# Down projection of a gated MLP: eight block products replaced by seven, with other loads and queues

## Chip, core and metric

One NeuronCore of a Trainium2 chip runs the whole program; the seven others do not take part. The metric is the device time of one execution in microseconds (us). Engines are named as in the profile: PE is TensorE (matmul), PEld its weight loads, DVE is VectorE, ACT is ScalarE, POOL is GpSimd, SP is SyncE, which here only issues DMAs.

## What is computed

One layer of a hybrid diffusion backbone for 2048 latent tokens and 128 context tokens with D_MODEL 1024 and D_FF 2816. A mixing sub-layer comes first, then a gated MLP. The change touches only the last two lines of the MLP:

```python
h = rmsnorm(x, g_pre_ffn) * (1.0 + scale_f) + shift_f
gt, up = jnp.split(h @ w_up, 2, axis=-1)
gt = (dwconv2d_grid(gt, conv_ffn) if grid else dwconv1d(gt, conv_ffn[1])) + b_conv_ffn
y = (jax.nn.silu(gt) * up) @ w_down          # (2176 x 2816) @ (2816 x 1024)
x = x + gate_f * rmsnorm(y, g_post_ffn)
```

All data is float32.

## The kernel before

The program is one `hybrid_step_kernel` that goes through five stages. Stages 1 to 3 (input projection, DeltaNet, output projection) end with `d_x2`, the residual stream, in DRAM. Stage 4 computes the up projection in two passes `p` over the two halves of the latent tokens, 22 column groups `j` in each. A `unit(p, j)` is seven products of 12 matmuls (a seven-product block scheme for `w_up`); `gate(p, j)` is the 3x3 depthwise convolution on DVE, SiLU on ACT and the product with the up branch, and it writes `d_y` (17 tiles of 128 tokens x 22 groups of 128 features) to DRAM. The operands of the unit lie in tiles T0 to T6 of 16 KB a partition, made in the order 0, 5, 4, 6, 1, 2, 3, which is also the order in which the last unit uses them for the last time.

Every float32 operand of a matmul is split into a high part (a copy rounded to float32r, by ACT) and a low part (a subtraction, by DVE or POOL), and one block product is three matmuls: high x high, high x low, low x high. One matmul has a 128x128 stationary piece of the activations and a 128x512 moving piece of the weights.

Stage 5 (lines 1463 to 1543) is the down projection and the end of the layer. `load_wd` (1469) makes the split weights of one k (128 rows of `w_down`, 512 columns) in 22 tiles `wd0` to `wd21`. `down_mm` (1475) takes a tile `c` of 128 tokens: for each half `q` of the 22 groups it loads 704 KB of `d_y` into `yt` (1478, SP's queue), splits it into `yr` (ACT 1480, DVE 1481), and issues 33 matmuls (1484 to 1486). The outer loop runs over the two column halves `hf`. For `hf` 0 the squares are summed (ACT 1524) and the result is copied to `half` (DVE 1526). For `hf` 1 all 22 weight tiles are made anew (loads 1512), and behind each token tile stand the root (1529), the reciprocal (1530), two scalings (DVE 1535, 1537), the addition of `d_x2` (loaded at 1533, added at 1539) and the store (1543, for the context tile 1541). All stage-5 DMAs are issued by SP. The first two token tiles use PSUM banks of stage 4, since the last `gate(1, 21)` is issued only after the split of tile 1 (`issue_after(last_v)`, 1497).

Tiles come from pools with a fixed number of buffers; a new use of a buffer waits for the last use of the old one. The framework writes the semaphores and puts the instructions of each engine in an order that it plans ahead, by program order and by the times that it expects; on the chip each engine and each queue then runs in that order.

## Time and profile before

| | us |
|---|---|
| median of three runs | 2793.51 (2789.07 to 2797.16) |
| the profiled execution | 2791.89 |
| its span (first to last instruction) | 2790.1 |
| stage 5: first to last matmul start | 2268.96 to 2781.93 |

| engine | busy us | share of the span | instructions |
|---|---|---|---|
| PE | 2654.8 | 95% | 15309 |
| DVE | 1907.2 | 68% | 2840 |
| ACT | 1153.1 | 41% | 2421 |
| POOL | 789.9 | 28% | 851 |

Matmuls are pipelined, so the duration of one in the records (391 ns) is longer than the distance from one to the next; where a rate is wanted, the starts are to be compared. A row of the timeline has the start, the duration, engine, line, operation, output <- inputs, and in brackets how long the engine had been idle and what ended that. PEclk is the granted clock of TensorE as a share of 2.4 GHz.

### The profile page before, as it was taken

The numbers are of one execution on the slowest core, as the hardware profiler recorded it, in microseconds if no ns is written. First come the engines' busy times: TensorE is split into PE (matmuls) and PEld (weight loads), VectorE is DVE, ScalarE is ACT, GpSimd is POOL, SyncE is SP. The second block draws the span as 40 slices with busy tenths as digits, with TensorE's granted clock in tenths as the row PEclk, the third lists the DMA queues.
The fourth block names the chain that finished last, engine by engine and source line by source line (L and its number), as shares of the span: only waits on it lengthen the run. The fifth ranks groups of instructions, "written<-read, shape, count | busy, mean of one in ns | idle before, by whom it ended". The sixth has DMA issues, their size and how long they took to land.

```text
span 2790.1 us, 41624 instructions
## 1 busy us (share of the span) xinstructions
PE 2654.8 (95%) x15309; PEld 2237.8 (80%) x15309; DVE 1907.2 (68%) x2840; ACT 1153.1 (41%) x2421; POOL 789.9 (28%) x851
## 2 busy tenths in 40 slices
PE   7999999979888998999899999999999999999998
PEld 4888888767778887888788888888888878888887
DVE  3898999885657785444687777887888873225343
ACT  5423132355656666666544444432222232224221
POOL 2211011166335683222666666500000000000000
PEclk9999999989969999999999999999999999999999
DMA  7024531576597565665777777888777754236453
GB/s 275 20 72 119 151 109 43 104 190 134 154 279 195 141 227 207 219 231 184 256 278 266 265 271 262 279 263 255 235 232 222 230 184 134 94 104 211 165 173 119
DMA packets 426712, 526.79 MB, mean 189 GB/s; under 512 B 144790, under 2 KB 301964, under 8 KB 426252
## 3 DMA queue, kind: packets, MB, share of 16 engines
q1 hardware_dynamic: 406380, 506.30, 57.5%
q10 hardware_dynamic: 20128, 17.83, 1.9%
q8 instruction: 121, 1.98, 0.3%
q14 instruction: 83, 0.68, 0.1%
HBM read 342.13 MB, written 181.90 MB: 188 GB/s over the span
## 4 chain that ended last, share of the span: by engine, by line
PE 61%; DMA 5%; DVE 4%; ACT 3%; SPq 3%; POOL 2%; issue 2%; ACTq 0%; DVEq 0%; POOLq 0%
PE ps L1318 10%; PE ps L1320 10%; PE ps L1319 10%; PE ps L1147 7%; PE ps L1486 6%; PE ps L1484 6%; PE ps L1485 6%; PE psc L1232 2%; SPq L166 1%; DVE dm L819 1%; PE p L938 1%; PE p L945 1%; DMA dm<-d_g 1%; DMA d_mix<-bigB 1%; PE p L957 1%
## 5 line engine op out<-in xcount | busy, mean ns | idle before, releaser
L1377 DVE SCALAR_TENSOR_TENSOR pa<-gb,pvf,pa 128x512 f32<-128x512 f32 (+1 forms) x704 | 491.0, 733 | 65.3 <-ACT pa L1375 62.5
L1318 PE MATMUL ps<-T,wr 128*128 128x512 f32 x1232 | 480.5, 391 | 0.1
L1319 PE MATMUL ps<-T,wr 128*128 128x512 f32 x1232 | 479.9, 389 | 0.0
L1320 PE MATMUL ps<-T,wr 128*128 128x512 f32 x1232 | 479.0, 390 | 0.6 <-POOL wr L1246 0.6
L361 PE MATMUL ps<-hH,wr 128*128 128x512 f32 (+1 forms) x960 | 349.7, 369 | 6.6 <-ACT bigA L412 3.8
L362 PE MATMUL ps<-hL,wr 128*128 128x512 f32 (+1 forms) x960 | 352.4, 367 | 0.0
L363 PE MATMUL ps<-hH,wr 128*128 128x512 f32 (+1 forms) x960 | 350.6, 366 | 0.0
L1484 PE MATMUL ps<-wd,yr 128*128 128x512 f32 x748 | 292.5, 391 | 6.1 <-ACT yr L1480 5.5
L1486 PE MATMUL ps<-wd,yr 128*128 128x512 f32 x748 | 292.1, 391 | 0.4 <-DVE yr L1481 0.4
L1485 PE MATMUL ps<-wd,yr 128*128 128x512 f32 x748 | 292.1, 391 | 0.0
L1318 PEld LDWEIGHTS ps<-T,wr 128*128 128x128 f32 x1232 | 231.4, 188 | 49.2 <-issue 0.8
L1320 PEld LDWEIGHTS ps<-T,wr 128*128 128x128 f32 x1232 | 231.4, 188 | 49.1 <-POOL wr L1246 1.1
L1319 PEld LDWEIGHTS ps<-T,wr 128*128 128x128 f32 x1232 | 231.4, 188 | 47.4
L375 DVE SCALAR_TENSOR_TENSOR acc<-bigA,pvt,acc 128x1024 f32<-128x1024 f32 (+2 forms) x168 | 252.3, 1502 | 13.2 <-ACT acc L372 9.2
L361 PEld LDWEIGHTS ps<-hH,wr 128*128 128x128 f32 x960 | 184.0, 193 | 33.5 <-ACT bigA L412 4.2
L1481 DVE TENSOR_TENSOR yr<-yt,yr 128x1408 fp32r<-128x1408 f32 x68 | 110.5, 1625 | 143.4 <-ACT yr L1480 143.3
L363 PEld LDWEIGHTS ps<-hH,wr 128*128 128x128 f32 x960 | 185.4, 193 | 25.4 <-issue 3.0
L362 PEld LDWEIGHTS ps<-hL,wr 128*128 128x128 f32 x960 | 185.3, 193 | 24.0 <-issue 1.6
L1351 POOL TENSOR_TENSOR up<-up,x 128x512 f32<-128x512 f32 x44 | 57.3, 1302 | 413.2 <-ACT pa L1383 217.9
L375 DVE SCALAR_TENSOR_TENSOR acc<-bigC,pvt,acc 128x1024 f32<-128x1024 f32 (+2 forms) x108 | 156.6, 1461 | 24.9 <-DMA bigB<-d_uc 15.5
L1484 PEld LDWEIGHTS ps<-wd,yr 128*128 128x128 f32 x748 | 141.0, 188 | 36.6 <-ACT yr L1480 6.5
L1486 PEld LDWEIGHTS ps<-wd,yr 128*128 128x128 f32 x748 | 141.0, 188 | 30.7 <-DVE yr L1481 1.4
(360 smaller groups left out, 4571.2 us busy)
## 6 DMA issues: line engine op xcount, KB each, us to landing
d_w<-wr SPq DMA_DIRECT2D x154, 512.0 KB
wr<-d_w SPq DMA_DIRECT2D x154, 512.0 KB
yt<-d_y SPq DMA_DIRECT2D x68, 704.0 KB
raw<-in_wup_dram SPq DMA_DIRECT2D x60, 512.0 KB
xt<-in_x_dram SPq DMA_DIRECT2D x34, 512.0 KB
wmt<-in_wmod_dram SPq DMA_DIRECT2D x24, 512.0 KB
wt<-in_win_dram SPq DMA_DIRECT2D x24, 512.0 KB
wmt<-in_wmod_dram SPq DMA_DIRECT2D x48, 256.0 KB
```

The source lines that it names most:

```text
L361: nc.tensor.matmul(ps[:, 0:n], wr[:, 0, k], hH[bi][:, k], start=(k == 0), stop=False)
L362: nc.tensor.matmul(ps[:, 0:n], wr[:, 0, k], hL[bi][:, k], start=False, stop=False)
L363: nc.tensor.matmul(ps[:, 0:n], wr[:, 1, k], hH[bi][:, k], start=False, stop=(k == KD - 1))
L375: nc.vector.scalar_tensor_tensor(dst, src[:, o + t:o + t + n], w[:, t:t + 1], dst, ALU.mult, ALU.add)
L1147: nc.tensor.matmul(pss[hf][:], a[:, k], w[k][:, 512 * hf:512 * hf + 512], start=(w is woH and a is mH and k == KD - 1), stop=(w is woL and ...
L1318: nc.tensor.matmul(ps[:], h, T[i][:, 0, k], start=(first and k == 0), stop=False, skip_group_check=True)
L1319: nc.tensor.matmul(ps[:], h, T[i][:, 1, k], start=False, stop=False, skip_group_check=True)
L1320: nc.tensor.matmul(ps[:], l, T[i][:, 0, k], start=False, stop=(k == HK - 1), skip_group_check=True)
L1377: nc.vector.scalar_tensor_tensor(rows(a), src, w[:, t:t + 1], rows(a), ALU.mult, ALU.add)
L1484: nc.tensor.matmul(ps[:], yr[:, 0, i], wd[:, 0], start=(q == 0 and i == 0), stop=False)
L1485: nc.tensor.matmul(ps[:], yr[:, 0, i], wd[:, 1], start=False, stop=False)
L1486: nc.tensor.matmul(ps[:], yr[:, 1, i], wd[:, 0], start=False, stop=(q == 1 and i == HN - 1))
```

## The change

The product Y W is cut into 2x2 blocks: Y by token half (tiles 0 to 7 and 8 to 15) and by half of the 22 groups, W by the same half of its rows and by column half. Seven products of sums and differences of blocks take the place of eight. The context tile belongs to the first token half and has no partner, so it takes part in products 1, 3, 5 and 7 only. The products run in the order 3, 1, 5, 6, 2, 4, 7; a unit `(i, c)` is one product for one token tile, 33 matmuls.

- `y_load` loads one or two blocks of `d_y` for a unit, each in two parts of 6 and 5 groups, two units ahead, on SP's queue into 8 buffers. `y_prep` adds or subtracts the two blocks (DVE) and splits (ACT, DVE), one unit ahead.
- `w_load` loads one or two 256 KB blocks of `w_down` per k, `w_make` adds or subtracts them (DVE) and splits (ACT; DVE or POOL). There are 15 weight buffers: 11 for the product that runs, 4 for the next. The other 7 are made as the last unit of a product frees them. From product 1 on, `w_load` is issued on POOL's queue into 3 buffers.
- `evict` copies (ACT) or adds or subtracts (DVE) the result of a unit into one or two of the accumulators `C1`, `C2` in SBUF.
- `final` has the work of the old lines 1524 to 1543, now from the accumulators, after each unit of product 4 (tiles 8 to 15) and of product 7 (tiles 0 to 7 and the context tile). The additions of `d_x2` go to POOL, but for tile 7 and the context tile, and the stores to POOL's queue.
- The pool `sp4` of stage 4 is closed after the first pass.

```diff
+        yq = s5.enter_context(tc.tile_pool(name="yq", bufs=8, reuse_waits="tile"))
+        yp = s5.enter_context(tc.tile_pool(name="yp", bufs=4, reuse_waits="tile"))
+        wpa = s5.enter_context(tc.tile_pool(name="wp5a", bufs=15, reuse_waits="tile"))
...
+        YS = {1: ((0, 0), (1, 1), ADD), 2: ((1, 0), (1, 1), ADD), 3: ((0, 0),), 4: ((1, 1),),
+              5: ((0, 0), (0, 1), ADD), 6: ((1, 0), (0, 0), SUB), 7: ((0, 1), (1, 1), SUB)}
+        WS = {1: ((0, 0), (1, 1), ADD), 2: ((0, 0),), 3: ((0, 1), (1, 1), SUB), 4: ((1, 0), (0, 0), SUB),
+              5: ((1, 1),), 6: ((0, 0), (0, 1), ADD), 7: ((1, 0), (1, 1), ADD)}
+        CS = {3: ((0, 1, None), (1, 1, None)), 1: ((0, 0, None), (1, 1, ADD)), 5: ((0, 0, SUB), (0, 1, ADD)),
+              6: ((1, 1, ADD),), 2: ((1, 0, None), (1, 1, SUB)), 4: ((0, 0, ADD), (1, 0, ADD)), 7: ((0, 0, ADD),)}
+        ORDER = (3, 1, 5, 6, 2, 4, 7)
+        units = [(i, c) for i in ORDER for c in list(range(8)) + ([CTX] if i in (1, 3, 5, 7) else [])]
+        KA = 6
+        PARTS = ((0, KA), (KA, HN - KA))
...
+        def y_prep(u):
+            yrs[u] = []
+            for (k0, kn), ts in zip(PARTS, yts.pop(u)):
+                if len(ts) == 2:
+                    nc.vector.tensor_tensor(ts[0], ts[0], ts[1], YS[u[0]][2])
+                yr = yp.tile([P, 2, KA, P], F32R, name="yr", tag="yr")
+                nc.scalar.copy(yr[:, 0, 0:kn], ts[0])
+                v = nc.vector.tensor_tensor(yr[:, 1, 0:kn], ts[0], yr[:, 0, 0:kn].bitcast(F32), SUB).ins
...
+        def w_load(i, k):
+            ws = wsp[0].tile([P, KD, P], F32, name="raw", tag="raw")[:].rearrange("p (a b) c -> p a (b c)", a=2)
+            t = [x for x in WS[i] if type(x) is tuple]
+            if len(t) == 2 and t[0][0] == t[1][0]:
+                wq[0].dma_start(ws, wdown[t[0][0] * HN + k].rearrange("p (a c) -> p a c", a=2))
+            else:
+                for n, (kh, h) in enumerate(t):
+                    wq[0].dma_start(ws[:, n], wdown[kh * HN + k, :, 512 * h:512 * h + 512])
...
+        def w_make(i, k, eng):
+            ws = wss.pop((i, k))
+            if len(WS[i]) == 3:
+                nc.vector.tensor_tensor(ws[:, 0], ws[:, 0], ws[:, 1], WS[i][2])
+            wd = wpa.tile([P, 2, 512], F32R, name="wd", tag="wd")
+            nc.scalar.copy(wd[:, 0], ws[:, 0])
+            eng.tensor_tensor(wd[:, 1], ws[:, 0], wd[:, 0].bitcast(F32), SUB)
...
+        y_load(units[0])
+        y_load(units[1])
+        y_prep(units[0])
+        AH = 3
+        for k in range(AH):
+            w_load(3, k)
+        for k in range(HN):
+            if k + AH < HN:
+                w_load(3, k + AH)
+            w_make(3, k, nc.vector if k % 2 == 0 else nc.gpsimd)
...
+        def final(t):
+            square(t, 0)
+            nc.vector.tensor_tensor(ss[:, t, 2:3], ss[:, t, 0:1], ss[:, t, 1:2], ADD)
+            nc.scalar.activation(ss[:, t, 3:4], ss[:, t, 2:3], AF.Sqrt, scale=1.0 / D, bias=epsb[:])
+            nc.vector.reciprocal(ss[:, t, 3:4], ss[:, t, 3:4])
+            xt = xts.pop(t)
+            G = Gs
+            if t == CTX:
+                G = fo.tile([P, D], F32, name="xt5", tag="xt5")
+                nc.sync.dma_start(G[:], d_gm[1][:, D:2 * D].to_broadcast([P, D]))
+            for h in range(2):
+                sl = slice(512 * h, 512 * h + 512)
+                nc.vector.scalar_tensor_tensor(C[h][:, t], C[h][:, t], ss[:, t, 3:4], G[:, sl],
+                                               ALU.mult, ALU.mult)
+                (nc.vector if t in (7, CTX) else nc.gpsimd).tensor_tensor(xt[:, sl], xt[:, sl], C[h][:, t], ADD)
+            nc.gpsimd.dma_start(y_prompt[0] if t == CTX else y_sample[0, t * P:(t + 1) * P, :], xt[:])
...
+        FREE = 15 - HN
+        wq[0] = nc.gpsimd
...
+        for n in range(3, len(units)):
...
+            t = {4: c + 8, 7: c}.get(i)
+            if t is not None:
+                x_load(t)
+            if n + 2 < len(units):
+                y_load(units[n + 2])
+            if n + 1 < len(units):
+                y_prep(units[n + 1])
+            if nxt:
+                for k in range(made[nxt], min(loaded[nxt], FREE, FREE if last else FREE * m // 5)):
+                    w_make(nxt, k, nc.gpsimd)
+                    made[nxt] += 1
+                load_to(nxt, made[nxt] + 3)
+            ps = pmm.tile([P, 512], F32, name="ps5", tag="mm")
+            mm(u, ps)
+            evict(u, ps)
...
+            if t is not None:
+                final(t)
+            if nxt and last:
+                for k in range(made[nxt], HN):
+                    w_make(nxt, k, nc.vector if k % 2 else nc.gpsimd)
+                    load_to(nxt, k + 4)
```

## Rows read from the trace of the kernel before

**Rows 1.** First part of the page: busy time of each engine.
```profile
PE 2654.8 (95%) x15309; PEld 2237.8 (80%) x15309; DVE 1907.2 (68%) x2840; ACT 1153.1 (41%) x2421; POOL 789.9 (28%) x851
```

**Rows 2.** Stretches: length, busy PE, PEld, DVE, ACT, POOL, clock, DMA share, GB/s.
```profile
2100.00:2200.00 100.00, 100.00 (x442) 82.81 (x442) 87.36 (x163) 26.92 (x48) 7.30 (x6) 1.00 0.72 225
2270.00:2280.00 10.00, 9.56 (x34) 7.60 (x34) 7.01 (x10) 5.21 (x9) 0.00 (x0) 0.77 1.03 395
2500.00:2600.00 100.00, 99.42 (x437) 81.55 (x436) 48.24 (x58) 36.17 (x52) 0.00 (x0) 1.00 0.59 195
2560.00:2780.00 220.00, 220.00 (x972) 182.20 (x971) 90.01 (x103) 49.24 (x71) 0.00 (x0) 1.00 0.48 160
```

**Rows 3.** Timeline of PE where stage 4 ends and stage 5 begins.
```profile
2263.03 0.39 PE L1320 MATMUL ps<-T,wr 128*128 128x512 f32 x1
2268.96 0.79 PE L1484 MATMUL ps<-wd,yr 128*128 128x512 f32 x1 [5.55 <-ACT yr L1480]
2270.62 0.79 PE L1486 MATMUL ps<-wd,yr 128*128 128x512 f32 x1 [0.44 <-DVE yr L1481]
...
2274.63 0.40 PE L1486 MATMUL ps<-wd,yr 128*128 128x512 f32 x1
...
2275.33 0.39 PE L1486 MATMUL ps<-wd,yr 128*128 128x512 f32 x1
...
2277.37 0.39 PE L1486 MATMUL ps<-wd,yr 128*128 128x512 f32 x1
```

**Rows 4.** Timelines of SP and ACT at the same place.
```profile
2263.45 0.80 SPq L1478 DMA_DIRECT2D yt<-d_y  x2
...
2267.55 1.36 ACT L1480 CAST yr<-yt 128x1408 fp32r<-128x1408 f32 x1 [1.11 <-DMA yt<-d_y]
```

**Rows 5.** Groups of stage 5 by shape: count, busy us, mean ns, idle before.
```profile
L1484 PE MATMUL ps<-wd,yr 128*128 128x512 f32 x748 | 292.5, 391 | 6.1 <-ACT yr L1480 5.5 <-ACT wd L1471 0.5
...
L1481 DVE TENSOR_TENSOR yr<-yt,yr 128x1408 fp32r<-128x1408 f32 x68 | 110.5, 1625 | 143.4 <-ACT yr L1480 143.3
L1480 ACT CAST yr<-yt 128x1408 fp32r<-128x1408 f32 x68 | 93.1, 1369 | 170.4 <-PE ps L1486 93.2 <-issue 75.7 <-DMA yt<-d_y 1.5
...
L1539 DVE TENSOR_TENSOR ot<-ot,xt 128x1024 f32<-128x1024 f32 x17 | 20.8, 1225 | 0.6
...
L1472 DVE TENSOR_TENSOR wd<-ws,wd 128x512 fp32r<-128x512 f32 x22 | 14.2, 687 | 7.2 <-ACT wd L1471 7.2
...
L1471 ACT CAST wd<-ws 128x512 fp32r<-128x512 f32 x22 | 13.1, 620 | 9.5 <-DMA ws<-in_wdown_dram 9.2
L1535 DVE SCALAR_TENSOR_TENSOR ot<-half,ss,G 128x512 f32<-128x512 f32 x17 | 12.8, 753 | 0.6
```

**Rows 6.** Timelines of SP and ACT at the change of the column half.
```profile
2522.86 6.00 SPq L1512 DMA_DIRECT2D ws<-in_wdown_dram  x5
...
2527.15 0.62 ACT L1471 CAST wd<-ws 128x512 fp32r<-128x512 f32 x1 [4.05 <-DMA ws<-in_wdown_dram]
```

**Rows 7.** One line of the code: duration of its instructions, ns min/median/max.
```profile
L247 SPq DMA_DIRECT2D G<-d_gm x2: 327/710/1092, 1100.0 to 2311.9; - x2
L1305 DVE TENSOR_TENSOR ts<-raw,ts x22: 683/685/1773, 1359.5 to 1766.4; 128x512 f32<-128x512 f32 x22
```

**Rows 8.** Timelines of POOL and DVE in stage 4, one place where both work.
```profile
1370.92 1.30 POOL L1246 TENSOR_TENSOR wr<-raw,wr 128x512 fp32r<-128x512 f32 x1
...
1370.99 1.77 DVE L1305 TENSOR_TENSOR ts<-raw,ts 128x512 f32<-128x512 f32 x1 [1.83 <-POOL wr L1246]
```

**Rows 9.** Timeline of the end.
```profile
2781.93 0.39 PE L1486 MATMUL ps<-wd,yr 128*128 128x512 f32 x1
2782.35 0.60 ACT L1524 ACTIVATE junk<-ps 128x512 bf16<-128x512 f32 x1 [12.82 <-PE ps L1486]
...
2785.24 1.23 DVE L1539 TENSOR_TENSOR ot<-ot,xt 128x1024 f32<-128x1024 f32 x1
2786.49 0.34 SPq L1541 DMA_DIRECT2D out_dram<-ot  x1
```

More of the change, by code (lines that the diff above doesn't have):

```diff
@@ L1475, in down_mm @@
-        def down_mm(c, ps):
-            for q in range(2):
-                yt = yq.tile([P, HN, P], F32, name="yt", tag="yt")
-                nc.sync.dma_start(yt[:], d_y[c, :, q * HN:(q + 1) * HN, :])
-                yr = yp.tile([P, 2, HN, P], F32R, name="yr", tag="yr")
-                nc.scalar.copy(yr[:, 0], yt[:])
-                v = nc.vector.tensor_tensor(yr[:, 1], yt[:], yr[:, 0].bitcast(F32), ALU.subtract).ins
-                for i in range(HN):
-                    wd = wds[q * HN + i]
-                    nc.tensor.matmul(ps[:], yr[:, 0, i], wd[:, 0], start=(q == 0 and i == 0), stop=False)
-                    nc.tensor.matmul(ps[:], yr[:, 0, i], wd[:, 1], start=False, stop=False)
-                    nc.tensor.matmul(ps[:], yr[:, 1, i], wd[:, 0], start=False, stop=(q == 1 and i == HN - 1))
-            return v
@@ new lines, in hybrid_step_kernel, with y_load @@
+        KA = 6
+        PARTS = ((0, KA), (KA, HN - KA))
+        wsp, wq = [rp], [nc.sync]
+        yts, yrs, wss, wds = {}, {}, {}, {}
+        def y_load(u):
+            i, c = u
+            t = [x for x in YS[i] if type(x) is tuple and (c != CTX or x[0] == 0)]
+            yts[u] = []
+            for k0, kn in PARTS:
+                yts[u].append([])
+                for r, q in t:
+                    yt = yq.tile([P, KA, P], F32, name="yt", tag="yt")[:, 0:kn]
+                    nc.sync.dma_start(yt, d_y[c if r == 0 else c + 8, :, q * HN + k0:q * HN + k0 + kn, :])
+                    yts[u][-1].append(yt)
@@ new lines, in evict @@
+        def evict(u, ps):
+            i, c = u
+            for r, h, op in CS[i]:
+                if c == CTX and r == 1:
+                    continue
+                d = C[h][:, c if r == 0 else c + 8]
+                if op is None:
+                    nc.scalar.copy(d, ps[:])
+                else:
+                    nc.vector.tensor_tensor(d, d, ps[:], op)
+        y_load(units[0])
[4 more added lines that the diff above has]
+            w_load(3, k)
@@ L1502, in hybrid_step_kernel @@
         fo = s5.enter_context(tc.tile_pool(name="fo", bufs=2, reuse_waits="tile", side="right"))
[L1503 to L1504 removed]
+        wsp[0] = s5.enter_context(tc.tile_pool(name="ws5", bufs=3, reuse_waits="tile", side="right"))
+        pmm = s5.enter_context(tc.tile_pool(name="pmm5", bufs=8, reuse_waits="tile", space=PSUM))
+        C1 = wp.tile([P, NT, 512], F32, name="C1")
```

104 lines of the change are left out of this document (48 added, 56 removed).

## Prediction

> **What bounds the kernel now.** The first part of the page comes first: PE is busy 95% of the span, DVE 68%, ACT 41% [rows 1]. The stretches then tell whether that holds where the change is made. In stage 5 PE is busy throughout at full clock, while DVE works 0.41 of the time, ACT 0.22, POOL not at all and the DMA engines 0.48 (stretch 2560 to 2780) [rows 2]. So PE sets the pace of stage 5, and what a matmul costs there decides. The 391 ns of the groups [rows 5] is not that cost, because matmuls overlap: the starts 2275.33 and 2277.37 lie nine matmuls apart, 2.04/9 = 0.227 us each [rows 3]. The 17 x 2 x 66 = 2244 matmuls of the stage should take 508.7 us; they take 2781.93 + 0.23 - 2268.96 = 513.2. The difference and the gap ahead of it are lost in two places. At the start, PE is free at 2263.26 and its twelfth matmul starts at 2274.63 where it could have started at 2265.75: 8.9 us lost, 5.7 of it waiting and the rest in waits and at the lower clock (nine starts in 4.01 us, 0.45 each; the granted clock of 2270 to 2280 is 0.77, so part of it was at the 1.2 GHz level after an idle PE) [rows 2, 3]. The reason is the first load of activations: SP issues it at 2263.45, right after the last matmul of stage 4, and ACT gets the data at 2267.55 [rows 4]. At the change of the column half 437 matmuls stand where a full stretch has 442: 5 x 0.227 = 1.1 us [rows 2].
>
> **The change part by part.** The sum is made against the profiled execution, 2791.9 us, of which 2790.1 is span. The median is 1.6 above it, and I add that at the end.
>
> *Matmuls.* Products 1, 3, 5 and 7 have 9 units, 2, 4 and 6 have 8: 60 units of 33, so 1980. 264 fewer at 0.227: **-59.9**. A unit lasts 7.48 us.
>
> *Start.* The buffers of `yq` and `yp` now come first in memory, 48 KB, over T0, T5 and T4, which the last unit of stage 4 uses first; three sevenths of a unit that ends at 2263.26 are past near 2252. The loads, ACT's cast and DVE's split of unit 0 can then lie beside the remaining products. The weights lie over T6, T1 and T2, free one after the other until 2260.5, and k 0 to 3 are loaded ahead in four buffers. From k = 4 on a load waits for a buffer, and load (4.3, below), difference, copy and split take some 6.5 us; the last k would come about 1.5 us after PE wants it. So 8.9 - 1.5: **-7.4** (-8.9 to 0, if the order planned for the queues holds the load back after all). The gate of group 21 is still queued on DVE behind a split, that of unit 3; PE then has units in hand, as before.
>
> *The old weight change* goes: **-1.1**.
>
> *Six new changes of weights.* Let T be the start of the last unit of a product. k = 4 of the next product needs the buffer that the first three matmuls free at T + 0.7. The copy is 0.62 [rows 5], the split on POOL 1.30 [rows 8]: T + 2.6. That frees one of three load buffers for k = 7. No row shows a DMA issued by POOL; SP's issues take 0.33 to 1.09 us [rows 7, 9], and I take the range for POOL. From issue to landing I take 4.3, the 256 KB load issued at 2522.86 and used at 2527.15, behind a load of activations [rows 6]. Then DVE's addition 0.69, copy 0.62, split 0.69 [rows 5]: k = 7 is made at T + 9.5, in time for T + 7.5 + 7 x 0.68 = T + 12.2. But the load of k = 10 starts only then: T + 9.5 + 0.7 + 4.3 + 2.6 = T + 17.1, and PE wants it at T + 14.3. A stall of 2.8 where the pair needs two DMAs (into products 1 and 4), 2.2 where one DMA brings both (into 6 and 7), 0.8 with a single block (into 5 and 2): 12 in all. With 1.09 for each issue, and four loads and two splits in one POOL queue, it is about 6 for each change, 36. Since the old change lost only 1.1 with 22 weights, the low end is 3; less than nothing it can't be, since PE has no loss there now. Nearer to the rows of SP and to the old change: **+17** (3 to 36).
>
> *Steady work beside PE.* Two points on one line, 512 elements in 687 ns and 1024 in 1225 [rows 5], give 0.96 and 0.82 us for the two parts of a tile. A unit with two blocks costs DVE 3.55, one with a single block 1.78. DVE adds evictions (0.69 each, 1 or 2 a unit) and 11 weight additions in a product; per unit it reaches 6.1 of 7.48 in products 5, 4 and 7. ACT stays under 5. So neither is the bound alone, but there is a catch: with POOL working, a 0.69 us operation of DVE took 1.77, begun 0.07 after one of POOL's [rows 8], and the largest of its line is 1.773 against a median of 0.685 [rows 7]. Operations of DVE and POOL that both read SBUF stand one behind the other. In product 4 these are 1.78 for the split, 1.2 for weights and two scalings of 0.75 on DVE, and on POOL 1.3 for a weight and 2.6 for the additions of `d_x2`: 8.4 us a unit against 7.48, up to 0.9 x 8 = 7 us. Product 7 has 7.7, nearly even. `x_load` stands ahead of `y_load` on SP and waits for a buffer that is free only when a store has landed, some 11 us after its unit; that takes up most of the two units' lead of the activations. I take **+6** (0 to 20) for products 4 and 7.
>
> *DMA bytes.* 101 loads of 704 KB, 132 blocks of 256 KB, 34 of 512 KB for `d_x2` and the stores, and the gates: 126 MB against 79. PE's pace asks for 193 to 334 GB/s by product (4 and 7 most). The same kinds of transfer moved 395 GB/s while they had the engines full (2270 to 2280) [rows 2]. So nothing is charged, with some margin even at 334.
>
> *Evictions, squares, closing a pool* cost nothing: there are eight PSUM banks for results, and ACT and DVE have room as counted.
>
> *End.* Now 8.0 us lie between the last matmul's end and the end of the span [rows 9]. After the change the last tile is first added up (0.69), scalings and additions on DVE stay, but its gate is loaded into a buffer of `xt5` that is free only when the store of tile 7 has landed: about 2 us after the last matmul, then some 4 for the load, and the scaling and additions (2.9), the issue and a store (3.3) follow: 12 to 13. **+4** (0 to 8).
>
> Sum: -59.9 - 7.4 - 1.1 + 17 + 6 + 4 = -41.4, so 2750.5, and on the median's footing 2752.
>
> **A rule weighed.** The Trainium skill, page "DMA: Bandwidth & Descriptors" (Specifications), puts the first byte of a GpSimd-issued DMA at about 1 us against 0.6 from the sync queue; no row here shows either. By it each of the two chained loads of a change would be 0.4 later, by my estimate 5 us for six changes, and the sum 2757.
>
> **The rivals.** *All waits are hidden*: the changes cost 3, products 4 and 7 nothing, the start gains 8.9, the end 2: -59.9 - 8.9 - 1.1 + 3 + 2 = -65, 2728. For it speaks the old change, which remade twice as many weights for 1.1 us; against it the three load buffers in a chain. *POOL's loads stand behind DVE*: POOL's queue runs splits, additions and DMA issues in order, and each may wait up to 1.1 us for a DVE operation [rows 8]. Five such waits in the chain of a change make 5.5 more: +33, and with 15 in products 4 and 7, 2791.9 - 68.4 + 36 + 15 + 6 = 2780, 2782 at the median's footing. The Trainium skill, page "SBUF — State Buffer" (Who interferes with whom), says that a GpSimd DMA starves while DVE holds the shared ports in a 2-port mode, and infers that `tensor_tensor` spares the descriptors; by that the splits wait, but the issues do not. *The activations arrive too late*, the slower side: parts of 2.5 and 3 KB a row in place of 5.5 KB, with two more queues. From 2263 to 2790 less 10 for the end, 126 MB fit if 244 GB/s are held; below that the kernel is slower than before. The stretch 2100 to 2200 moved 225, but at a share of 0.72 [rows 2]; if that were all there is, stage 5 would take 560 us and the kernel 2836. Against it speaks 395 GB/s at a full share.
>
> **How the numbers follow.** My forecast (2735 to 2770) 0.50; all hidden 0.17; POOL behind DVE (2770 to 2785) 0.20; a mixture that lands within 0.3% 0.05; activations late 0.08. 0.3% (8 us) is about what a measurement of this kernel can tell from no change. Faster 0.87, same 0.05, slower 0.08. The range takes in the first three but for their tails: 2728 to 2785. The predicted time is 2752.
>
> **What would show it.** Matmuls of stage 5: 1980 at 0.227. The first of them within 2 us of stage 4's last: start right. Gaps of PE at the third part of the first unit of a product, released by a `wd` of k 8 to 10: changes right; gaps released by `yr` in products 4 and 7: the steady part. Durations of DVE's two-input operations above their medians where POOL works: the catch. A DMA share near 1 with PE waiting for `yt` over whole products would make the prediction wrong, and so would a lower clock over more than the first microseconds.

## The result and the profile after

The changed kernel takes 2823.14 us (median, 2816.05 to 2826.37), the kernel before 2791.29 beside it: a ratio of 1.0126, interval 1.0100 to 1.0153. It is slower; the prediction said 2752, at most 2785. The profiled execution is 2823.96 us, its span 2822.1.

The page's first part, busy time of each engine:

```profile
PE 2615.8 (93%) x15045; PEld 2190.1 (78%) x15045; DVE 2054.4 (73%) x3046; ACT 1189.3 (42%) x2540; POOL 970.5 (34%) x1039
```

Two stretches: length, busy PE, PEld, DVE, ACT, POOL, clock, DMA share, GB/s. The first is stage 5 from its first to its last matmul, the second the change of weights into product 7.

```profile
2257.00:2795.00 538.00, 479.69 (x1980) 382.19 (x1980) 344.17 (x433) 175.20 (x313) 176.24 (x185) 0.94 0.69 224
...
2706.00:2742.00 36.00, 22.94 (x70) 16.24 (x69) 28.42 (x31) 7.11 (x14) 17.03 (x16) 0.72 0.76 258
```

PE's total fell by 39 us against [rows 1], as it had less to multiply, but its share fell too: PE is idle for 58 us of the 538 in stage 5, and some more runs at the lower clock (0.94). The DMA engines are not full. What PE waited for in stage 5 is the next view (who waited, for whom, us in total, times, longest).

```profile
PE ps L1536 <- DVE wd L1527: 22.1, 8, 6.3
PE ps L1537 <- DVE yr L1507: 14.8, 12, 4.8
PE ps L1535 <- ACT yr L1506: 9.8, 3, 4.2
PE ps L1535 <- DVE acc L1384: 9.2, 1, 9.2
PE ps L1536 <- POOL wd L1527: 2.4, 2, 2.1
PE ps L1535 <- ACT wd L1526: 1.7, 2, 1.2
```

For a balance, cut the matmuls in their order into groups of 33, one for each unit (neighbouring units overlap a little), and take the distance between the starts of successive groups; what it has over 33 x 0.2267 = 7.48 us is the unit's loss, with what the low clock behind a wait costs. Units of a product are counted from 0. Stage 5 is counted from the end of stage 4's last matmul. Before: 526.8 = 508.7 of matmuls + 10.2 lost (8.9 at the start, the rest nearly all at the old change) + 7.9 behind the last matmul. After: 567.2 = 448.9 + 91.0 + 27.3. "Changes" are the first two units of products 1, 5, 6, 2, 4 and 7, and the context unit ahead of them; "rest" is all other units.

| | forecast | measured |
|---|---|---|
| matmuls | -59.9 | -59.8 |
| start, lost | 1.5 | 7.6 |
| units 2 to 4 of product 3 | 0 | 12.6 |
| changes of weights | 17 (3 to 36) | 59.7 |
| rest | 6 (0 to 20) | 11.2 |
| behind the last matmul | 12 | 27.3 |

Stage 5 is 40.4 us longer. In the profiled execution the part ahead of it was 8.3 us shorter (2254.92 against 2263.26). In the kernels below that point lies between 2247 and 2264, and it moves with the distance of the profiled execution from its kernel's median: 2247 in experiment 8, 15 us below its median, and 2262 in experiment 14, 12 us above. So I read stage 5 on its own and leave those 8 us unexplained.

### The profile page after: what moved, and what is told of

It is laid out like the page before. It is cut to its first block, busy times and chain, and to the rows that moved or that the text cites. A ratio compares the mean times of both kernels' runs of the same rounds, so it can differ in the third digit from the quotient of the medians.

```text
span 2822.1 us, 42083 instructions
## 1 busy us (share of the span) xinstructions
PE 2615.8 (93%) x15045; PEld 2190.1 (78%) x15045; DVE 2054.4 (73%) x3046; ACT 1189.3 (42%) x2540; POOL 970.5 (34%) x1039
## 4 chain that ended last, share of the span: by engine, by line
PE 47%; DMA 14%; DVE 9%; issue 3%; SPq 3%; ACT 3%; POOL 2%; DVEq 0%; POOLq 0%; ACTq 0%
PE ps L1318 10%; PE ps L1320 10%; PE ps L1319 10%; DMA yt<-d_y 6%; PE ps L1147 6%; PE psc L1232 2%; DVE yt L1504 2%; PE ps L1535 1%; PE ps L1537 1%; PE ps L1536 1%; SPq L166 1%; DMA dm<-d_g 1%; DMA raw<-in_wdown_dram 1%; DVE dm L819 1%; PE p L945 1%
## 5 line engine op out<-in xcount | busy, mean ns | idle before, releaser
L1536 PE MATMUL ps<-wd,yr 128*128 128x512 f32 x660 | 265.7, 404 | 24.6 <-DVE wd L1527 22.1
L1535 PE MATMUL ps<-wd,yr 128*128 128x512 f32 x660 | 262.1, 404 | 20.7 <-ACT yr L1506 9.8
L1537 PE MATMUL ps<-wd,yr 128*128 128x512 f32 x660 | 265.2, 403 | 14.8 <-DVE yr L1507 14.8
L1504 DVE TENSOR_TENSOR yt<-yt 128x768 f32<-128x768 f32 x82 | 80.7, 984 | 140.1 <-DMA yt<-d_y 140.0
L1536 PEld LDWEIGHTS ps<-wd,yr 128*128 128x128 f32 x660 | 128.6, 195 | 57.6 <-DVE wd L1527 26.4
L1535 PEld LDWEIGHTS ps<-wd,yr 128*128 128x128 f32 x660 | 128.9, 195 | 51.3 <-ACT yr L1506 11.5
```

Of the source, the lines that this page charges most:

```text
L1535: nc.tensor.matmul(ps[:], h, wd[:, 0], start=(k == 0), stop=False)
L1536: nc.tensor.matmul(ps[:], h, wd[:, 1], start=False, stop=False)
L1537: nc.tensor.matmul(ps[:], l, wd[:, 0], start=False, stop=(k == HN - 1))
```

## The experiments

All are the changed kernel with an edit, but for the one that repeats it; each ran beside the kernel before, which took 2783 to 2786 us there, so the ratios are to be compared and not the times. The table has each kernel's ratio and the balance of its profiled execution. The planner orders all engines anew for every edit, so a place far from the edit moves by some us; changes and rest are best read as a sum. Experiments 1, 6 and 9, whose edits lie elsewhere, have 62.2, 68.3 and 67.4 there against 70.9, so a few us of difference in it show nothing.

| kernel | ratio (95%) | start | units 2-4 | changes | rest | end | stage 5 |
|---|---|---|---|---|---|---|---|
| changed | 1.0126 (1.0100-1.0153) | 7.6 | 12.6 | 59.7 | 11.2 | 27.3 | 567.2 |
| changed, again | 1.0132 (1.0105-1.0159) | 7.2 | 12.4 | 54.7 | 17.5 | 27.5 | 568.1 |
| 1 PSUM | 1.0100 (1.0066-1.0134) | 7.6 | 1.4 | 43.3 | 18.9 | 29.6 | 549.5 |
| 2 order | 1.0050 (1.0026-1.0074) | 6.4 | 13.6 | 39.7 | 0.0 | 25.9 | 534.4 |
| 3 stores on SP | 1.0106 (1.0078-1.0134) | 6.5 | 13.6 | 48.3 | 12.5 | 20.6 | 550.3 |
| 4 one part | 1.0139 (1.0106-1.0172) | 8.4 | 5.5 | 49.9 | 33.0 | 19.0 | 564.6 |
| 5 weights on SP | 1.0062 (1.0042-1.0083) | 7.5 | 12.6 | 41.6 | 11.1 | 22.7 | 544.3 |
| 6 end buffers | 1.0090 (1.0058-1.0122) | 7.4 | 12.5 | 53.8 | 14.5 | 17.4 | 554.4 |
| 7 half the activations | 1.0045 (1.0028-1.0063) | 7.6 | 12.6 | 31.9 | 9.6 | 27.6 | 538.0 |
| 8 = 1+2+3+6 | 0.9974 (0.9956-0.9992) | 7.8 | 1.4 | 45.8 | 1.6 | 8.8 | 514.1 |
| 9 start order | 1.0134 (1.0110-1.0157) | 10.8 | 8.4 | 51.3 | 16.1 | 27.3 | 562.7 |
| 10 four load buffers | 1.0030 (1.0015-1.0046) | 7.1 | 10.8 | 37.6 | 6.0 | 21.9 | 532.2 |
| 11 = 8+5 | 0.9956 (0.9939-0.9972) | 7.5 | 1.4 | 48.9 | 2.2 | 8.9 | 517.6 |
| 12 = 8+9+10 | 0.9918 (0.9899-0.9936) | 11.2 | 2.0 | 26.1 | 0.0 | 9.2 | 497.3 |
| 13 = 8+10, end work | 0.9907 (0.9879-0.9936) | 7.6 | 4.1 | 23.0 | 1.6 | 9.4 | 494.4 |
| 14 = 13, memory | 0.9876 (0.9849-0.9903) | 5.8 | 3.8 | 27.8 | 2.5 | 9.4 | 498.2 |
| 15 = 13, DVE only | 0.9912 (0.9881-0.9943) | 6.4 | 4.0 | 29.3 | 3.5 | 9.2 | 501.3 |
| 16 = 2+10 | 0.9951 (0.9938-0.9965) | 7.4 | 10.8 | 27.2 | 2.1 | 18.8 | 515.1 |
| 17 = half of 10, separate buffers | 1.0068 (1.0043-1.0093) | 6.4 | 12.0 | 17.9 | 28.0 | 29.7 | 542.8 |

**Without an edit.**

> The changed kernel once more, without an edit, on the chip of these runs. It tells how far its losses vary from one execution to another: kernels whose edit lay elsewhere lost 43 to 54 us at the changes of weights, it lost 59.7. If this spread is the chip's, this run lies anywhere between 43 and 60; if it is the planner's (each edit makes it draw another order for all engines), it repeats 58 to 61. The time should be 1.010 to 1.015 of the kernel before.

Stage 5 repeats within 0.9 us, changes and rest together within 1.3 (70.9, 72.2). The changes alone, 54.7, lie below the 58 to 61 that the planner as the only cause would give: between the two columns some us move from one execution to the next.

**1, PSUM.** The timeline of PE in the changed kernel has one wait of 9.16 us. The expectation calls the place unit 3; it is the 133rd matmul of the stage, so the first of unit 4:

```profile
2303.09 0.79 PE L1535 MATMUL ps<-wd,yr 128*128 128x512 f32 x1 [9.16 <-DVE acc L1384]
```

```diff
-        pmm = s5.enter_context(tc.tile_pool(name="pmm5", bufs=8, reuse_waits="tile", space=PSUM))
+        pmm = s5.enter_context(tc.tile_pool(name="pmm5", bufs=4, reuse_waits="tile", space=PSUM))
```

> The PSUM pool of stage 5 gets 4 buffers in place of 8, as the kernel before had; nothing else. In the changed kernel (2823.1 us) the first matmul of unit 3 waits 9.2 us for DVE's L1384, the last convolution group of stage 4. Theory A (the eight-buffer pool lies over the two banks that the convolution still uses, so unit 3 waits for it): the wait goes and the time is 2811 to 2816. Theory B (DVE is busy with the convolution and the split activations of unit 3 come late with any bank): PE waits for yr there instead, 2821 to 2826.

The wait is gone from the list of what PE waited for (experiment 1, the whole of stage 5):

```profile
PE ps L1537 <- DVE yr L1507: 20.2, 12, 4.5
PE ps L1535 <- ACT yr L1506: 8.6, 4, 3.3
PE ps L1536 <- DVE wd L1527: 5.2, 3, 2.6
PE ps L1535 <- ACT wd L1526: 3.9, 3, 2.1
PE ps L1536 <- POOL wd L1527: 3.0, 4, 1.9
```

11.2 us at the place itself; theory A. Experiments 8 and 11 to 15, which have the edit, show no such wait either. By the ratio, from the mean 1.0129 of the two runs of the changed kernel to 1.0100, it is 8 us.

**2, order.** The change into product 1 shows what DVE does while PE waits for weights (timelines of DVE, ACT and PE, the changed kernel; in brackets the idle time and its end):

```profile
2347.73 0.96 DVE L1504 TENSOR_TENSOR yt<-yt 128x768 f32<-128x768 f32 x1 [4.84 <-DMA yt<-d_y]
...
2351.74 0.82 DVE L1504 TENSOR_TENSOR yt<-yt 128x640 f32<-128x640 f32 x1 [2.32 <-DMA yt<-d_y]
2352.49 0.69 DVE L1527 TENSOR_TENSOR wd<-raw,wd 128x512 fp32r<-128x512 f32 x1
...
2362.63 0.82 DVE L1504 TENSOR_TENSOR yt<-yt 128x640 f32<-128x640 f32 x1 [4.58 <-DMA yt<-d_y]
2363.37 0.68 DVE L1527 TENSOR_TENSOR wd<-raw,wd 128x512 fp32r<-128x512 f32 x1
...
2336.71 1.67 ACT L1526 CAST wd<-raw 128x512 fp32r<-128x512 f32 x3
...
2358.08 0.62 ACT L1526 CAST wd<-raw 128x512 fp32r<-128x512 f32 x1 [13.52 <-DVE raw L1524]
...
2353.23 0.79 PE L1536 MATMUL ps<-wd,yr 128*128 128x512 f32 x1 [6.29 <-DVE wd L1527]
2364.11 0.50 PE L1536 MATMUL ps<-wd,yr 128*128 128x512 f32 x1 [3.15 <-DVE wd L1527]
```

ACT has cast the weights by 2358.70, so their split could run. DVE stands idle for 4.58 us ahead of an addition of activations whose load hasn't landed; by its place in the row of additions it is that of unit (1, 4), while PE is at (1, 1). The split follows at once, 4.7 us late, and PE's matmul 0.06 us behind it. The split before it, at 2352.49, for which PE waited 6.29 us, was later still: it is that of k = 5 (POOL splits the even k, and PE's wait is at the 17th matmul of the unit), whose cast is the second of three from 2336.71. From the last unit of a product to the end of the next one's first, DVE waited 37.6 us in this way over the six changes.

PE pays twice here, for behind the wait of 6.29 us it runs at the lower of its two levels, 1.2 GHz (length, busy PE, PEld, DVE, ACT, POOL, clock, DMA share, GB/s):

```profile
2353.20:2358.00 4.80, 4.77 (x11) 3.80 (x12) 3.09 (x4) 0.00 (x0) 2.12 (x4) 0.50 0.74 196
```

Its matmuls start 0.43 us apart there. Behind the 3.33 us that it waited for weights into product 5 it stayed at 1.00 (2431.50 to 2436.00). Of the 59.7 us of the changes PE stood idle for 39; most of the rest is matmuls at the lower clock.

```diff
-                y_prep(units[n + 1])
+                with tc.issue_after(lastw) if lastw is not None else ExitStack():
+                    y_prep(units[n + 1])
+                lastw = None
...
-                    w_make(nxt, k, nc.vector if k % 2 else nc.gpsimd)
+                    v = w_make(nxt, k, nc.vector if k % 2 else nc.gpsimd)
+                    lastw = v if k % 2 else lastw
```

> In the first unit of products 1, 5, 6, 2, 4 and 7 the additions and splits of the next unit's activations are put behind the last weight split that DVE makes for the new product. Changes of weights lose about 59 us of PE in the changed kernel (2823.1 us). Theory A (DVE keeps a fixed order in which an addition of activations that still waits for its load stands ahead of weights that PE wants now): the changes fall to 20 to 30 us and the time to 2785 to 2800. Theory B (the three load buffers and POOL's queue make the weights late, the order on DVE does not matter): 2815 to 2830.

Changes and rest together went from 71 to 40, the time by 22 us (1.0129 to 1.0050). That is theory A, though the changes stayed above its 20 to 30: into products 1, 5, 6 and 2 they went from 39.3 to 20.4, into product 7 only from 20.4 to 18.6. The edit holds back ACT's casts of these activations too; the rows above are what points to DVE.

**7, half the activations.** The second loads are left out:

```diff
-                for r, q in t:
+                for r, q in t[:1]:
...
-                    yts[u][-1].append(yt)
+                    yts[u][-1] += [yt] * len(t)
```

> In the units with two blocks of activations only the first block is loaded, and it is added to (or subtracted from) itself: the second loads are left out, so the result is another. All instructions of DVE, ACT, POOL and PE stay. With 8 buffers the loads are then twice as far ahead. Theory A (DVE's additions wait 140 us in all for activations, and what stands behind them in DVE's order, weights and splits, comes late to PE): the waits go, the changes of weights fall from 59 to 15 to 25 us and the waits for split activations from 25 to under 5; 2760 to 2780. Theory B (the chain of three weight buffers on POOL's queue binds at the changes): 2805 to 2815.

Between the two: 23 us by the ratio, changes 31.9. And the reason given for A failed: with half the loads DVE's additions still waited 109.9 us, where they had waited 140.0 (at the changes 25.8, where it was 37.6). What DVE waited for in the changed kernel, then the same row of experiments 7 and 16, of which more below:

```profile
DVE yt L1504 <- DMA yt<-d_y: 140.0, 64, 6.3
```

```profile
DVE yt L1504 <- DMA yt<-d_y: 109.9, 58, 10.7
```

```profile
DVE yt L1504 <- DMA yt<-d_y: 49.4, 36, 6.0
```

A wait of DVE costs PE only where something urgent is queued behind it. That the order matters more than the amount of loads is not shown by this pair: both edits shortened DVE's waits and the time.

**10 and 17, buffers.** Four load buffers need 4 KB; the room came from giving each of the two parts of the activations buffers of its own, of its exact size (separate rings):

```diff
-        yq = s5.enter_context(tc.tile_pool(name="yq", bufs=8, reuse_waits="tile"))
-        yp = s5.enter_context(tc.tile_pool(name="yp", bufs=4, reuse_waits="tile"))
+        yq = s5.enter_context(tc.tile_pool(name="yq", bufs=4, reuse_waits="tile"))
+        yp = s5.enter_context(tc.tile_pool(name="yp", bufs=2, reuse_waits="tile"))
...
-                    yt = yq.tile([P, KA, P], F32, name="yt", tag="yt")[:, 0:kn]
+                    yt = yq.tile([P, kn, P], F32, name="yt", tag=f"yt{k0}")[:]
...
-                yr = yp.tile([P, 2, KA, P], F32R, name="yr", tag="yr")
+                yr = yp.tile([P, 2, kn, P], F32R, name="yr", tag=f"yr{k0}")
...
-        wsp[0] = s5.enter_context(tc.tile_pool(name="ws5", bufs=3, reuse_waits="tile", side="right"))
+        wsp[0] = s5.enter_context(tc.tile_pool(name="ws5", bufs=4, reuse_waits="tile", side="right"))
...
-                load_to(nxt, made[nxt] + 3)
+                load_to(nxt, made[nxt] + 4)
...
-                    load_to(nxt, k + 4)
+                    load_to(nxt, k + 5)
```

> Four weight load buffers in place of three and one more load ahead; the memory comes from separate buffers for the two parts of the activations (4 + 4 and 2 + 2 of their exact size, so the lead of the activations stays two units). Theory A (the prediction's chain of buffers: load, addition, cast and split through three buffers): the changes of weights, 59.7 us, fall by 10 to 20. Theory B (the order on DVE holds the weights up, not the buffers): they fall by 0 to 5.

28 us by the ratio, so theory A seemed right. Experiment 17 has only the first half of the edit:

> Separate buffers for the two parts of the activations (4 and 4 to load, 2 and 2 split, of their exact size), with three weight load buffers as in the changed kernel. Theory A (in the kernel with four weight buffers it was the weight buffers that helped): changes of weights 48 to 60, 2810 to 2825. Theory B (the separate rings helped, since a load of one part no longer waits for a buffer of the other): 36 to 45, 2790 to 2805.

The changes fell to 17.9 with three load buffers, while the rest rose to 28.0: together 45.9 against 43.6 with the fourth buffer. So what the edit did at the changes is owed to the separate rings; the fourth buffer is worth 11 us by the ratios (1.0068 to 1.0030, intervals that just overlap), not at the changes; in the profiles 7.8 of it lie at the end (29.7 to 21.9). Theory A of experiment 10 falls. Why separate rings help, with the same lead of two units, no run shows: the planner's order is another with them, too.

**16, order and buffers together.**

> Only two edits of the changed kernel: the later activations behind the last weight split on DVE, and four weight load buffers (with separate buffers for the two parts of the activations). Alone they left 39.7 and 37.6 us at the changes of weights, where 59.7 were. Theory A (two separate causes): 20 to 28 at the changes, and the time 40 to 50 us below the changed kernel's, 2770 to 2785. Theory B (the same cause, mended twice): 33 to 40 and 2790 to 2800.

50 us below the changed kernel (1.0129 to 0.9951), 2770.25: theory A. Changes and rest fell from 71 to 29, and the waits of DVE for activations in the windows of the changes from 37.6 to 5.0. The changes into products 1, 5, 6 and 2 lost 11.0 in place of 39.3, that into product 7 still 15.3. These edits alone make it faster than the kernel before.

**3 and 6, the end.** The timeline of the end in the changed kernel, and then POOL's drains by line (count, duration ns min/median/max, first and last start):

```profile
2768.69 31.70 SPq L1588 DMA_DIRECT2D xt<-d_x  x7
...
2800.08 0.68 DVE L1548 TENSOR_TENSOR C<-C,ps 128x512 f32<-128x512 f32 x1
...
2805.54 0.32 SPq L1599 DMA_DIRECT2D xt<-d_gm  x1
...
2809.23 1.41 DVE L1602 SCALAR_TENSOR_TENSOR C<-C,ss,xt 128x512 f32<-128x512 f32 x2 [6.94 <-DMA xt<-d_gm]
...
2812.14 0.53 POOL L1605 DMA_DIRECT2D out_dram<-xt  x1 [11.15 <-DVE xt L1604]
```

```profile
L1719 POOLq DRAIN  x3: 40/102/9202, 2812.1 to 2821.8; - x3
```

The last matmul ends at 2794.8. The loads of `d_x2` for the last seven tiles stand behind all activations on SP and go through two buffers, the gate's load at the end of that chain. Then POOL's queue drains for 9.20 us from 2812.12, 6.0 longer than the last store takes to land (2815.28, when SP's drain comes).

```diff
-            nc.gpsimd.dma_start(y_prompt[0] if t == CTX else y_sample[0, t * P:(t + 1) * P, :], xt[:])
+            nc.sync.dma_start(y_prompt[0] if t == CTX else y_sample[0, t * P:(t + 1) * P, :], xt[:])
```

> The 17 stores of the result are issued by SP again; the weight loads stay on POOL's queue. The changed kernel (2823.1 us) ends with a drain of POOL's queue of 9.2 us, 6.0 of it after the last store has landed. Theory A (those 6 us belong to a queue of POOL that ends with a store): the end falls by 5 to 7 us, 2815 to 2819. Theory B (the stores only change the queue and the end waits as long on SP, or stores block the loads on SP): 2821 to 2828.

The end fell by 6.7, the time by 6 to 7 us: theory A in size. But a drain of 9.75 us is still there, begun earlier (2785.0) and hidden:

```profile
L1719 POOLq DRAIN  x3: 40/93/9749, 2785.0 to 2802.7; - x3
```

With only the stores on POOL's queue (experiment 5) it is 3.65 us, with no DMA on it (experiment 11) 2.43:

```profile
L1718 POOLq DRAIN  x3: 40/93/3646, 2787.5 to 2791.6; - x3
```

```profile
L1728 POOLq DRAIN  x3: 40/82/2427, 2753.6 to 2770.5; - x3
```

So the length goes with the 88 weight loads on that queue more than with the stores, and what moves the end is when POOL issues last.

```diff
+            if t in (1, 2, 4, 6, CTX):
+                xts[t] = wsp[0].tile([P, KD, P], F32, name="raw", tag="raw")[:].rearrange("p a c -> p (a c)")
...
+            if t == 6:
+                xts["G"] = wsp[0].tile([P, KD, P], F32, name="raw", tag="raw")[:].rearrange("p a c -> p (a c)")
+                nc.sync.dma_start(xts["G"], d_gm[1][:, D:2 * D].to_broadcast([P, D]))
...
-                G = fo.tile([P, D], F32, name="xt5", tag="xt5")
-                nc.sync.dma_start(G[:], d_gm[1][:, D:2 * D].to_broadcast([P, D]))
+                G = xts.pop("G")
```

> In product 7 the loads of d_x2 use the three weight load buffers, which are free by then, beside the two of their own, and the gate of the context tile is loaded with tile 6, not behind the store of tile 7. Theory A (the 27.3 us behind the last matmul are a chain of loads, additions and stores through two buffers, 5.2 us a tile, with the gate's load at its end): the end falls to 13 to 18 and the time to 2808 to 2814, against 2823.1. Theory B (the end is set by DVE's and POOL's work and the drain of POOL's queue): 2820 to 2826.

The end is 17.4, the ratio 11 us lower: theory A. With both edits (experiment 8) it is 8.8, near the 7.9 of before [rows 9].

**4, one part.**

```diff
-        yq = s5.enter_context(tc.tile_pool(name="yq", bufs=8, reuse_waits="tile"))
-        yp = s5.enter_context(tc.tile_pool(name="yp", bufs=4, reuse_waits="tile"))
+        yq = s5.enter_context(tc.tile_pool(name="yq", bufs=4, reuse_waits="tile"))
+        yp = s5.enter_context(tc.tile_pool(name="yp", bufs=2, reuse_waits="tile"))
...
-        KA = 6
-        PARTS = ((0, KA), (KA, HN - KA))
+        KA = HN
+        PARTS = ((0, HN),)
```

> The activations of a unit are loaded and split in one piece of 11 groups again (704 KB a load, one cast and one split a unit, 4 load buffers and 2 split buffers in place of 8 and 4 of about half the size). Theory A (the two parts let loads, additions and splits of a later unit begin half a unit earlier, so undoing them makes DVE wait longer for loads): start +2, changes of weights +5 to +20, 2830 to 2850 against 2823.1. Theory B (the parts matter little, since the order on DVE and the lead of two units stay): 2816 to 2828.

2823.90, theory B: splitting in two parts, one of the change's other loads, gives nothing that can be measured here. It costs at unit 4 of product 3 and at the end what it saves elsewhere (changes and rest 82.9 against 71).

**5 and 11, the queue of the weight loads.**

```diff
-        wq[0] = nc.gpsimd
```

> The weight loads of products 1 to 7 are issued by SP, as in product 3; the stores stay on POOL's queue. Theory A (POOL's queue makes the weights late, since a load there waits behind splits, additions and stores): changes of weights 59 to 45 us, 2805 to 2815 against 2823.1. Theory B (on SP a weight load stands behind loads of activations that wait for a buffer which DVE frees, so the same late DVE delays it even more): 2828 to 2860.

19 us by the ratio, changes 41.6: theory A; 4.6 of it lie at the end, where the drain is shorter. On top of the four edits of experiment 8:

> The kernel with the four edits together, and besides the weight loads on SP, so that POOL issues no DMA. That kernel's stage 5 takes 514.1 us, 45.8 of it lost at changes of weights (16.5 into product 1, 17.5 into product 7). Theory A (what is left at the changes is POOL's order of splits, additions and loads, 0.55 us for each load): changes 20 to 30, stage 5 490 to 502. Theory B (three load buffers are what is left, or SP's order of all loads and stores is as bad): stage 5 510 to 530.

Changes 48.9, stage 5 517.6: theory B, and the ratio is that of experiment 8 within the intervals. With those edits in, the queue of the weight loads makes no difference that can be measured; which of them takes its gain away no run shows.

**8 and 12, together.**

> The four edits together: 4 PSUM buffers, the later activations behind the last weight split on DVE, stores by SP, the buffers and the early gate in product 7. Stage 5 from the end of stage 4 took 526.8 us in the kernel before and 567.2 in the changed one. If the causes are separate (gate -11, order -31, queue of the stores -9 at the last change, drain -6, chain of the end -7 to -10): 500 to 512, that is 15 to 27 us faster than the kernel before. If they share one resource (the transfers, which take longer when more of them run at once): 525 to 540, not faster than before.

The single gains by ratio were 8, 22, 6 and 11, 47 in all; together 43. So the causes hardly overlap. Stage 5 is 514.1, 2 us above theory A's range; 2778.68, barely faster than the kernel before.

> The kernel with the four edits together, and besides the fourth weight load buffer and the order at the start; weight loads stay on POOL. Theory A (with the order on DVE mended, the chain of three buffers is what is left of the changes): changes 45.8 to 20 to 30, start 7.8 to 4, stage 5 490 to 502. Theory B (POOL's queue is what is left): changes 40 to 46, stage 5 504 to 512.

Changes 26.1, stage 5 497.3, as theory A has it but for the start; by experiment 17 the rings are the likelier cause than the fourth buffer. 2761.90.

**9 and 14, the start.** PE and ACT where stage 5 begins in the changed kernel:

```profile
2254.70 0.39 PE L1320 MATMUL ps<-T,wr 128*128 128x512 f32 x1
2257.57 0.50 PE L1535 MATMUL ps<-wd,yr 128*128 128x512 f32 x1 [2.48 <-ACT yr L1506]
...
2260.08 0.80 PE L1537 MATMUL ps<-wd,yr 128*128 128x512 f32 x1 [1.79 <-DVE yr L1507]
...
2255.12 1.66 ACT L1526 CAST wd<-raw 128x512 fp32r<-128x512 f32 x3 [0.67 <-PE ps L1320]
2256.69 1.45 ACT L1506 CAST yr<-yt 128x768 fp32r<-128x768 f32 x2
```

Three weight casts wait for stage 4's last matmul (2255.08), and the activations stand behind them. PE then runs at the lower of its two levels, 1.2 GHz, for some 5 us (granted clock 0.50 in 2260 to 2265), as it did behind its wait in the kernel before [rows 2, 3].

```diff
-        y_prep(units[0])
+        a0, v0 = y_prep(units[0])
...
-            w_make(3, k, nc.vector if k % 2 == 0 else nc.gpsimd)
+            with tc.issue_after(a0), tc.issue_after(v0):
+                w_make(3, k, nc.vector if k % 2 == 0 else nc.gpsimd)
```

> At the start of stage 5 the weight casts and splits of product 3 are put behind the casts and splits of unit 0's activations on ACT and DVE. In the changed kernel PE lost 7.6 us here (2.6 ahead of the first matmul, 4.9 in the first unit), as much as before. Theory A (ACT's order puts four weight casts, which wait for stage 4's last matmuls to free their memory, ahead of activations that landed earlier): the loss falls to 2 to 4 us. Theory B (the weights come too late with either order): 6 to 9 us.

`a0` and `v0` are the last cast and the last split of unit 0. The loss is 10.8 and, in experiment 12, 11.2: worse than both theories have it, as PE now waited 4.3 us for the first weight split.

```diff
+        wpa0 = s5.enter_context(tc.tile_pool(name="wp5a0", bufs=1, reuse_waits="tile"))
...
-            wd = wpa.tile([P, 2, 512], F32R, name="wd", tag="wd")
+            s = len(wds) % 15
+            wd = (wpa0 if s < 4 else wpa).tile([P, 2, 512], F32R, name=f"wd{s}", tag=f"wd{s}")
```

> As the kernel with tile 15's end work behind the weights, and besides the first four weight buffers come first in memory, where the operands of stage 4 lie that its last unit uses first. Theory A (at the start the weight casts wait for stage 4's last matmul because their memory is used until then, and this is why the 7.6 us stayed): the loss at the start falls to 2 to 4. Theory B (what waits is the order of ACT and DVE, in which work of stage 4's last product stands ahead): 6 to 9.

5.8, between the two; the kernels with neither edit at the start have 6.4 to 8.4, so memory is a small part of it at most. ACT, then DVE, in experiment 14:

```profile
2260.52 2.17 ACT L1528 CAST wd<-raw 128x512 fp32r<-128x512 f32 x4
2262.60 2.81 ACT L1507 CAST yr<-yt 128x768 fp32r<-128x768 f32 x4
...
2262.40 2.83 DVE L1529 TENSOR_TENSOR wd<-raw,wd 128x512 fp32r<-128x512 f32 x2
2265.16 3.28 DVE L1508 TENSOR_TENSOR yr<-yt,yr 128x768 fp32r<-128x768 f32 x4
```

The weight casts now begin ahead of stage 4's last matmul (2261.37), but the activations still come behind them on ACT, and behind two weight splits on DVE. The edits of 9 and 14 were not tried together. 2750.00 is the fastest of these kernels, but its interval overlaps that of experiment 13, so no gain of this edit is shown.

**13 and 15, the change into product 7.** This one is different: in the changed kernel DVE waited only 1.3 us for activations there, yet 20.4 were lost. Timelines of DVE and POOL, where [rows 8] showed one such pair:

```profile
2710.98 1.74 DVE L1527 TENSOR_TENSOR wd<-raw,wd 128x512 fp32r<-128x512 f32 x1
2712.65 3.82 DVE L1592 TENSOR_TENSOR ss<-ss 128x1 f32<-128x1 f32 x1
...
2710.34 1.84 POOL L1527 TENSOR_TENSOR wd<-raw,wd 128x512 fp32r<-128x512 f32 x1
2712.13 0.57 POOL L1605 DMA_DIRECT2D out_dram<-xt  x1
2712.72 2.51 POOL L1604 TENSOR_TENSOR xt<-xt,C 128x512 f32<-128x512 f32 x2
2715.18 1.26 POOL L1527 TENSOR_TENSOR wd<-raw,wd 128x512 fp32r<-128x512 f32 x1
```

```diff
-            if t is not None:
+            if t is not None and not (nxt and last):
                 final(t)
...
+                if t is not None:
+                    with tc.issue_after(lastw):
+                        final(t)
```

> The kernel with the four edits and the fourth weight load buffer, with the changed kernel's own order at the start; besides, the root, scalings and additions of tile 15 (the last of product 4) are put behind the last weight split for product 7. With the order at the start in place of that edit, this kernel lost 15.3 us at the change into product 7 and 11.2 at the start, and its stage 5 took 497.3. Theory A (DVE's and POOL's end work of tile 15 stands ahead of the weights): the change into product 7 falls to 5 to 9, stage 5 is 483 to 490 with 7.6 at the start. Theory B (the end work of tile 14 and the exclusion of DVE and POOL hold it up as much): 12 to 16, stage 5 491 to 497.

12.9, theory B: it isn't tile 15's end work alone. 2757.01.

```diff
-                    v = w_make(nxt, k, nc.vector if k % 2 else nc.gpsimd)
+                    v = w_make(nxt, k, nc.vector)
```

> As the kernel with tile 15's end work behind the weights, and besides all late weights of a change are split on DVE, none on POOL. Theory A (with POOL beside it, an operation of DVE takes up to 1.8 us in place of 0.7, so POOL's splits cost DVE as much as they save): the changes stay or fall by 2 to 5 us against that kernel. Theory B (POOL's splits are a real help, DVE has 3 or 4 splits of 0.69 more in a row at each change): they rise by 5 to 12.

The changes rose by 6.3, with the rest by 8.2: theory B in the profile, though the times (2759.28 and 2757.01) can't be told apart. But the rise lies at the change into product 1 (5.0 to 12.2); into product 7 it is 12.1 in place of 12.9. So that POOL's splits help is not shown. What holds 12 to 15 us at this change is not settled: end work, additions and splits of DVE and POOL all meet there, and no edit took one away whole. Experiments 5 and 17, with other edits and another order, lost 8.6 there.

## Why the prediction was wrong, step by step

Stage 5 was to be 41.4 us shorter and is 40.4 longer, 81.8 off: 42.7 at the changes, 15.3 at the end, 12.6 at units 2 to 4, 6.1 at the start, 5.2 in the rest.

- *Matmuls*: 1980 at 0.2267; right, -59.8.
- *Start*: wrong in its first sentence. The loads were early (2248.74), but the step took the weights' casts to run ahead of stage 4's end, "free one after the other"; three of four waited for its last matmul [rows 3, 4 show the place before], and all four stood ahead of the activations. 7.6 in place of 1.5; the gain of 7.4 was 1.3. Experiment 14 let the casts run ahead and still lost 5.8: the order on ACT and DVE, which the step left out, is the likelier part, but no run shows it alone.
- *Old weight change*: went, as said.
- *Six changes*: the step that failed most. Its chain has each DVE operation run as soon as its input is there. DVE runs a planned order, and the plan put additions of activations, whose loads had not landed, ahead of weights that could be split. 59.7 and 54.7 in place of 17, above the 36 that was to bound it. The bound was made of POOL's queue and three buffers alone, and the fourth buffer didn't lower the changes. The chain's prices were near (an issue on POOL 0.54 us, a landing 4.9 in the median for the 4.3 taken), but it binds at k 8 to 10, and in products 1, 5, 6 and 2 PE's first wait is at k = 5, the first weight that DVE splits there. Into product 4, where the chain was to cost most and DVE has no activations to add, the change lost 0.0; into the others 14.6 (1), 7.8 (5), 8.9 (6), 8.0 (2) and 20.4 (7), and the cause of the last stays open. The lower clock behind some of the waits was priced at nothing too. With the order and the rings mended the changes cost 27.2.
- *Steady work*: 11.2 and 17.5, within 0 to 20, but by luck: the 6 was for products 4 and 7, and these lost 1.8 of the 11.2, product 6 lost 7.1. The exclusion of DVE and POOL was right as a mechanism, but its place is the change into product 7 more than the products themselves.
- *DMA bytes*: right. 224 GB/s at a share of 0.69, and experiment 13 moves the same bytes faster, at 0.75 (from the end of stage 4 to the last matmul):

```profile
2254.00:2739.00 485.00, 464.26 (x1981) 374.06 (x1980) 353.10 (x437) 178.90 (x316) 179.02 (x171) 0.98 0.75 253
```

- *Evictions and closing a pool at nothing*: wrong. "There are eight PSUM banks for results" counts two that the last convolution still held; 12.6, of which experiment 1 takes away 11.2.
- *End*: 27.3 in place of 12 to 13. The waiting for a buffer was seen for the gate alone; the seven loads of `d_x2` ahead of it were not counted, nor the drain of POOL's queue.

The rivals: "activations too late" had the right sign, but not by its mechanism: it asked for transfers that can't hold 244 GB/s, and 253 were held. Loads did land too late for DVE's order, but not for want of rate: in stage 5 SP waited 251.6 us for DVE to free their buffers (waits of SP, the changed kernel). More of these buffers were not tried.

```profile
SPq L1497 <- DVE yr L1507: 159.4, 99, 9.8
...
SPq L1497 <- DVE yt L1504: 92.2, 77, 6.4
```

"POOL's loads behind DVE" was right in part: the 256 KB loads of line 1518 waited 48.4 us in all for DVE's split of the buffer that they were to fill, and moving the loads to SP gave 19 us. The Trainium skill, page "SBUF — State Buffer" (Who interferes with whom), was cited for the splits waiting and the issues not; the trace agrees, POOL's 17 store issues took 0.53 to 0.58 us (median 0.57) throughout. The same section calls the lock on the shared ports exclusive; that agrees too, and here DVE waited for three instructions of POOL in a row.

The Trainium skill, page "PSUM — Partial Sum Buffer" (Engine vs sequencer instructions), says that the queues of ScalarE, VectorE and GpSimdE are strict FIFO. The trace agrees: DVE stood idle with a split ready to run. The prediction had the rule in words for POOL's queue and didn't apply it to DVE's.

The forecast of 2752, 0.985 of the time before, is near the kernels with all of this mended (0.9907 in experiment 13, 0.9876 in 14), but their stage 5 takes 494.4 and 498.2 us, where it had 526.8 - 41.4 = 485.4.

## What to carry to other kernels

An engine that runs a fixed order has to be costed in that order: for each operation that the bottleneck waits for, list what is queued ahead of it and what each of those waits for, loads above all. Counting an engine's busy share, or a chain of dependences without the queue, misses that. Where a pool of buffers takes over memory or PSUM banks, name the last user of each; and at the end of a kernel count every load through the buffers that the last tile shares.

## What the runs showed of the hardware

- POOL's drain at the end of the program lasts 9.20 to 9.75 us from when it is reached if POOL issued the 88 weight loads of stage 5 (with the stores or without them), 3.65 with 17 stores alone, 2.43 with no DMA. It shows at the end only if POOL's last issue is late.
- A two-input DVE operation of 128x1 took 3.82 us (2712.65), where the same line took 0.16 at the end of the program, while POOL did three operations in a row; DVE got no turn between them. It is 3.82 again in the second profiled execution. The longest in [rows 8] was 1.77.
- A DMA issue on POOL took 0.54 us (the 66 loads of 256 KB of line 1518, median) where SP's took 0.35 for the same line; POOL's landed 4.9 us after their issue (median, 2.8 to 8.8).
